# Where a fused decoder trunk gates and sums its output weights: one stage earlier, with three small moves in the attention

## The chip, the cores and the metric

The kernel runs on one core of one Trainium2 chip. The metric is the device time of one execution in microseconds (us). Three runs of the kernel before took 1230.39, 1235.14 and 1230.96 us; the median is 1230.96 us.

## What is computed

One decoder layer on x (1024 tokens x 1024 channels, float32): an adaLN-modulated RMSNorm, one combined input projection, two gated linear attentions side by side (HGRN2 with 8 heads, GLA with 4), a projection of each, a sigmoid gate on each, their sum, an output projection with a gate, a residual and a last RMSNorm.

```python
h = rms_norm(x, norm_w) * (1.0 + scale) + shift        # shift, scale, gate: silu(c) @ ada_w + ada_b
hq, hf, hi, hz, gq, gk, gv, gz, ga, mg = split(h @ w_in)
y_h = hgrn2_branch(hq, hf, hi, hz, lb, hgrn_norm_w)    # S_t = diag(f_t) S + (1 - f_t) i_t^T, norm, * silu(hz)
y_g = gla_branch(gq, gk, gv, gz, ga, ...)              # the same with alpha = sigmoid(W2 W1 x + b)^(1/16)
mg = sigmoid(mg)                                       # two gates per channel
merged = mg[0] * (y_h @ w_branch[0]) + mg[1] * (y_g @ w_branch[1])
x = x + gate * (merged @ w_out)
return rms_norm(x, final_norm_w)
```

The `gate` of the last line but one is a row over output channels, so the kernel multiplies it into the columns of `w_out` ahead of the product.

## The kernel before

**Arithmetic.** Every product is done in three matmuls on float32r parts: high times high, high times low, low times high. A tensor's high part is a rounding copy on ACT (`CAST` in the rows), its low part the difference, taken on DVE. Large projections use a Strassen-like scheme of seven products on half-size blocks, in the order `PRODUCTS = (1, 2, 5, 3, 6, 7, 4)`; weights of products 5, 6, 3 and 7 are sums of blocks.

**First two thirds.** After the norm, a stream of projections runs on TensorE (L541 and its neighbours), and the attention heads are woven in beside it: a head is a Python generator, and each `yield n` lets about n further units of stream matmuls be issued ahead of the next step of the head. In `attention` (L657) DVE prepares `xb` (L673 to L679), `yield 3` follows, then 32 pairs of score matmuls (L683). `inverse_root` (L957) splits a row of sums of squares into high and low parts (L197 on DVE is the low part) and multiplies both with ones (L964, L965). A second track prepares the weight sums (`ws`, L1200) and the factors of the activations (`fx`) in device memory.

**Last stages.** `last_stages` (L1388) runs four stages b = 0 to 3: the gate projection that goes with branch 1 (b = 0), the other gate (b = 1), the product of branch 1 (b = 2) and of branch 0 (b = 3). A stage is 7 products, a product is 4 pairs (i = 0 to 3), a pair is 12 matmuls (L1342) of 128 x 128 by 128 x 512. Weights come as "duos", two per product: loaded from device memory on SP's queue (L1273 for sums, L1277 for blocks of `w_in` or `w_branch`), cast on ACT (L1284), low part on DVE (L1285). `ahead` keeps duos loaded four and prepared two ahead. Activation factors are built by L1262 (ACT) and L1263 (DVE). Results leave PSUM as snapshots on ACT (L1314, L1316) and sums on DVE (L1329). The gate sigmoids (L1413) are stored through POOL's queue (L1414); put_gate0 (L1418) does the same without a store.

**Output weights.** `load_wy` (L1465) loads four 128 x 2 x 512 tiles of `w_out` (a half, kk), `gate_wy` (L1473) multiplies a tile by the gate, `sum_wy` (L1482) adds two, and `keep_wy` (L1468) stores a result, 512 KB each, through POOL's queue. `at` maps (stage, product, pair) to what is issued behind that pair. Before, both halves are in stage 1: half 0 is loaded behind product 2, gated in product 5, summed in product 3, half 1 loaded behind product 3, gated in product 6, summed in product 7; the tiles are freed at the last sum of their half.

**What sets the order.** Each engine works through its instructions in order. The tile framework orders them within an engine by its own scheduling, unless an instruction is kept in program order. All these tiles live in 46 equal slots of a FIFO (`N_SLOTS`): a slot freed is reused by the tile that asks next after all slots freed before it, and a load into it waits for the slot's last reader. PSUM banks of 512 columns are handed on through a list `R` (class Banks, L1289), too; before the last stages two 1024-column tiles are lent to it.

Of the kernel before, what the change touches and what calls it, by code (L numbers as in the profile page):

```python
# [15 lines left out]
P = 128  # L16
D = 1024
# [66 lines left out]
def hybrid_trunk_kernel(  # L84
# [20 lines left out]
    def dtile():  # L105
        cnt[0] += 1
        return ps_d.tile([P, T], F32, tag="d", name=f"pd{cnt[0]}")
# [548 lines left out]

    def attention(q, k, f, v, vo, V, post):  # L657

# [20 lines left out]
        TT(X[:, :, :, 4], X[:, :, :, 5], f4[:, :, :, 1], M)  # L679
        yield 3  # L680
        for b in range(32):
# [80 lines left out]
        grow(32)  # L762
        yield 7

# [192 lines left out]
    def inverse_root(dst, sq, n):  # L957

        hi, lo = split(sq)
        for half in range(2):  # L960
            sl = slice(half * 512, half * 512 + 512)
# [7 lines left out]
    def gla_attention(h):  # L969
# [16 lines left out]
        nc.gpsimd.tensor_add(sq[0], sq[0], sq[1])  # L986
        yield 2.5
        rst = sq[1]
        inverse_root(rst, sq[0], 256)
        for half in range(4):  # L990
# [94 lines left out]
    def hgrn_attention(h):  # L1085
# [4 lines left out]
        def post(vh, half, po):  # L1090
            if half == 0:
# [6 lines left out]
        yield from attention(st.pop(("q", h)), st.pop(("k", h)), st.pop(("f", h)), lambda: st[("v", h // 4)],  # L1098
                             h % 4 * P, P, post)
        if h % 4 == 3:  # L1100
# [7 lines left out]
        if h == 7:  # L1108
            yield 2
            rst = S.get([T])  # L1110
            inverse_root(rst, ssq[0], D)
            S.free(ssq[0])
            rst_h[0] = rst
# [356 lines left out]
    def gate_wy(kk, n):  # L1470
        kh, f = ((0, 0), (0, 1), (1, 0), (1, 1))[n]
        t = wy[kh, f]
        nc.vector.tensor_mul(t, t, gate_b[0][:, f * 512:f * 512 + 512].unsqueeze(1).to_broadcast([P, 2, 512]))  # L1473
        for p, at_ in X_OF.items():
# [5 lines left out]
    def sum_wy(kk, n):  # L1480
        p, dst, other = ((7, (0, 0), (0, 1)), (5, (0, 1), (1, 1)), (6, (1, 1), (0, 0)), (3, (1, 0), (1, 1)))[n]
        nc.vector.tensor_add(wy[dst], wy[dst], wy[other])  # L1482
        keep_wy(p, kk, *dst)
        if n == 3:
            S.free(*wy.values())
            wy.clear()

# [97 lines left out]

    for kk, (pa, pb) in enumerate(((5, 3), (6, 7))):
        after(1, 2 if kk == 0 else 3, 3, lambda kk=kk: load_wy(kk))
        for n in range(4):
            after(1, pa, n, lambda kk=kk, n=n: gate_wy(kk, n))
            after(1, pb, n, lambda kk=kk, n=n: sum_wy(kk, n))  # L1590

# [89 lines left out]
    S.free(*h_hi, *h_lo)  # L1681
    for _ in range(2):
        pd = dtile()
        R.lend([pd[:, 0:512], pd[:, 512:1024]])
    last_stages()
# [30 lines left out]
```

## Time and profile before

| | |
|---|---|
| runs | 1230.39, 1235.14, 1230.96 us |
| profiled execution | 1230.16 us, span 1228.3 us |
| mean granted TensorE clock | 0.993 |
| busy: PE, DVE, ACT, POOL | 1187.6, 791.6, 547.1, 123.7 us |
| DMA packets | 183.51 MB, 149 GB/s in the mean |
| `wo` stores (L1468) | 14 x 512 KB |
| gatings, sums of the output weights | 8 x 1.22 us from 904.2 us on, 8 x 1.225 us from 919.0 us on |

The profile names an instruction by its line, its engine and the tiles it writes and reads (`b` is any slot tile, `pd`, `pm` and `sc_ps` are PSUM, `ws`, `wo`, `fx`, `gate`, `yg`, `yh` tensors in device memory). A row of the timeline has start, duration, engine, line, operation, tiles, count, and in brackets how long the engine was idle before it and what ended that. Stage 0 begins beside the last attention head at 806.85 us, stage 1 begins at 899.33 us and its product 7 at 966.05 us.

### The profile page before, as it was taken

How to read it: one execution, taken by the hardware profiler on the slowest of the kernel's cores; microseconds unless marked ns; L12 is line 12 of the kernel's file. 1: busy time of each engine (PE TensorE's matmuls, PEld its weight loads, DVE VectorE, ACT ScalarE, POOL GpSimd, SP SyncE). 2: the span in 40 equal slices, each digit the busy share in tenths (PEclk: the TensorE clock that was granted, in tenths of full speed). 3: DMA queues.
4: the chain of work that ended last, by engine and by line, in shares of the span. 5: the costliest groups of instructions: out<-in, count | busy, mean ns of one | idle time of the engine just before them, and what ended most of it. 6: DMA issues, size and time to landing. Idle time of an engine off the chain costs nothing.

```text
span 1228.3 us, 20868 instructions
## 1 busy us (share of the span) xinstructions
PE 1187.6 (97%) x8579; PEld 984.7 (80%) x8579; DVE 791.6 (64%) x1245; ACT 547.1 (45%) x797; POOL 123.7 (10%) x215
## 2 busy tenths in 40 slices
PE   6999999999999999999999999999999699999997
PEld 3777889899898888788878878877888488878886
DVE  5636344774938465787774276785435666988994
ACT  5547723444444243324422334457632454544554
POOL 4100000202111112022010101011111000000000
PEclk9999999999999999999999999999999799999999
DMA  9714001845453367265151111245579736435533
GB/s 325 265 69 137 18 19 35 277 136 199 136 164 121 105 207 237 72 197 180 53 188 53 52 47 58 80 154 175 183 251 356 259 135 210 153 103 171 162 105 128
DMA packets 130961, 183.51 MB, mean 149 GB/s; under 512 B 7467, under 2 KB 97633, under 8 KB 130866
## 3 DMA queue, kind: packets, MB, share of 16 engines
q1 hardware_dynamic: 117250, 136.87, 35.4%
q0 software_dynamic: 13568, 45.31, 9.6%
q8 instruction: 67, 1.10, 0.4%
q14 instruction: 28, 0.23, 0.1%
q10 hardware_dynamic: 48, 0.01, 0.0%
HBM read 132.87 MB, written 49.28 MB: 148 GB/s over the span
## 4 chain that ended last, share of the span: by engine, by line
PE 51%; issue 29%; DVE 6%; POOL 3%; ACT 3%; DMA 3%; POOLq 0%; SPq 0%; DVEq 0%; ACTq 0%
PE pd L541 14%; PE pd L1342 7%; PE sc_ps L1342 4%; PE pm L1342 3%; PE pd L1517 3%; PE pd L643 2%; PE pd L645 2%; PE pd L644 2%; PE sc_ps L1517 2%; PE pd L352 1%; PE pm L848 1%; PE pm L1517 1%; PE pm L829 1%; PE pm L850 1%; POOL gate L1414 1%
## 5 line engine op out<-in xcount | busy, mean ns | idle before, releaser
L541 PE MATMUL pd<-b,b 128*128 128x512 f32 x1632 | 387.8, 394 | 0.0
L541 PEld LDWEIGHTS pd<-b,b 128*128 128x128 f32 x1632 | 302.3, 188 | 65.2 <-issue 1.4
L1342 PE MATMUL pd<-b,b 128*128 128x512 f32 x720 | 173.6, 392 | 2.4 <-DVE b L953 1.5
L1342 PEld LDWEIGHTS pd<-b,b 128*128 128x128 f32 x720 | 134.2, 188 | 33.3 <-DVE b L953 1.9
L197 DVE TENSOR_TENSOR b<-b,b 128x1024 fp32r<-128x1024 f32 (+2 forms) x89 | 99.1, 1124 | 83.4 <-ACT b L196 66.1
L196 ACT CAST b<-b 128x1024 fp32r<-128x1024 f32 (+2 forms) x89 | 82.9, 948 | 92.2 <-DVE b L1198 14.4
L1285 DVE TENSOR_TENSOR b<-b,b 128x1024 fp32r<-128x1024 f32 x56 | 68.4, 1224 | 52.2 <-ACT b L1284 19.6
L1342 PE MATMUL sc_ps<-b,b 128*128 128x512 f32 x324 | 81.8, 401 | 12.9 <-DVE b L1329 12.2
L1284 ACT CAST b<-b 128x1024 fp32r<-128x1024 f32 x56 | 58.3, 1049 | 75.5 <-PE pd L1342 19.1
L1342 PEld LDWEIGHTS sc_ps<-b,b 128*128 128x128 f32 x324 | 61.9, 193 | 27.4 <-DVE b L1329 12.6
L600 PE MATMUL pd<-b,b 128*128 128x256 f32 x256 | 74.2, 290 | 0.0
L1263 DVE TENSOR_TENSOR b<-b,b 128x1024 fp32r<-128x1024 f32 x48 | 59.5, 1254 | 21.7 <-ACT b L1262 14.3
L602 PE MATMUL pd<-b,b 128*128 128x256 f32 x256 | 72.5, 283 | 0.0
L601 PE MATMUL pd<-b,b 128*128 128x256 f32 x256 | 72.4, 283 | 0.0
L1342 PE MATMUL pm<-b,b 128*128 128x512 f32 x300 | 72.1, 389 | 0.0
L1262 ACT CAST b<-b 128x1024 fp32r<-128x1024 f32 x48 | 50.0, 1049 | 38.5 <-PE pd L1342 17.0
L1342 PEld LDWEIGHTS pm<-b,b 128*128 128x128 f32 x300 | 56.3, 188 | 11.7
L352 PE MATMUL pd<-b,b 128*128 128x512 f32 x192 | 53.2, 409 | 1.7 <-ACT b L196 0.9
L1200 POOL DMA_DIRECT2D ws<-b x64 | 34.6, 541 | 192.6 <-DVE b L1194 87.3
L643 PE MATMUL pd<-b,b 128*128 128x512 f32 x128 | 51.3, 401 | 0.0
L735 ACT COPY xb<-b 128x512 f32<-128x512 f32 x48 | 29.4, 620 | 48.2 <-PE sc_ps L715 26.3
L644 PE MATMUL pd<-b,b 128*128 128x512 f32 x128 | 49.9, 390 | 0.0
(285 smaller groups left out, 1965.4 us busy)
## 6 DMA issues: line engine op xcount, KB each, us to landing
b<-in_w_in_dram SPq DMA_DIRECT2D x66, 512.0 KB, 4.2
ws<-b POOLq DMA_DIRECT2D x64, 256.0 KB, 3.5
b<-ws SPq DMA_DIRECT2D x32, 512.0 KB, 4.1
b<-in_x_dram SPq DMA_DIRECT2D x16, 512.0 KB, 5.9
b<-in_ada_w_dram SPq DMA_DIRECT2D x32, 256.0 KB, 7.0
b<-in_w_branch_dram SPq DMA_DIRECT2D x16, 512.0 KB, 4.2
b<-h SPq DMA_DIRECT2D x14, 512.0 KB, 4.0
wo<-b POOLq DMA_DIRECT2D x14, 512.0 KB, 7.0
```

The source lines that it names most:

```text
L196: nc.scalar.copy(hi, src)
L197: nc.vector.tensor_sub(lo, src, hi.bitcast(F32))
L352: nc.tensor.matmul(accs[f], wg(a, d, f), b[d][:, half * 512:half * 512 + 512], start=(d == 0 and n == 0), stop=(d == KT - 1 and n == 2))
L541: nc.tensor.matmul(ps[0:w, th * 512:(th + 1) * 512], a[:, k, 0:w], b[:, th * 512:(th + 1) * 512], start=(k == 0 and n == 0), stop=(k == KT ...
L600: nc.tensor.matmul(o, lh, hi[:, k % 4, :], start=(k == 0), stop=False)
L601: nc.tensor.matmul(o, lh, lo[:, k % 4, :], start=False, stop=False)
L602: nc.tensor.matmul(o, ll, hi[:, k % 4, :], start=False, stop=(k == KT - 1))
L643: nc.tensor.matmul(o, lh, hi[:, k % 2, :], start=(k == 0), stop=False)
L644: nc.tensor.matmul(o, lh, lo[:, k % 2, :], start=False, stop=False)
L1285: nc.vector.tensor_sub(lo, t, hi.bitcast(F32))
L1342: nc.tensor.matmul(o, a[:, sl], c, start=(p in (1, 5) and kt == 0 and n == 0), stop=(kt == 3 and n == 2), skip_group_check=True)
L1517: nc.tensor.matmul(o, a, b, start=(p in (1, 5) and kt == 0 and n == 0), stop=(kt == 3 and n == 2), skip_group_check=True)
```

## The change

Four edits. The kernel's lines behind the split in inverse_root move down by one, those behind `gate_wy` by two and more.

1. Output weights: half 0 is loaded behind product 3, pair 0, of stage 0, gated in product 6 and summed in product 7 of stage 0; its tiles are freed behind the first pair of stage 1. Half 1 is loaded behind product 1, pair 2, of stage 1, gated in product 5 and summed in product 6, freed behind the last pair of product 7. Gatings and sums are kept in program order.
2. The two PSUM tiles are lent to `R` in reversed order.
3. `attention` gets an argument `lead`: heads 1 and 5 of HGRN issue their scores after `yield 4` and take `yield 6` in place of 7 later.
4. `inverse_root` is a generator with `yield 1` behind its split; GLA's `yield 2.5` ahead of it becomes 1.5.

```diff
--- before.py
+++ after.py
@@ -654,7 +654,7 @@
         return h_hi[k], h_lo[k]
 
 
-    def attention(q, k, f, v, vo, V, post):
+    def attention(q, k, f, v, vo, V, post, lead=3):
 
 
 
@@ -677,7 +677,7 @@
         TT(X[:, :, :, 1:4:2], q4[:, :, :, 2:4], f4[:, :, :, 2:4], M)
         TT(X[:, :, :, 2:6:3], X[:, :, :, 1:4:2], f4[:, :, :, 1:3], M)
         TT(X[:, :, :, 4], X[:, :, :, 5], f4[:, :, :, 1], M)
-        yield 3
+        yield lead
         for b in range(32):
             ch, j = b // 4, b % 4
             nc.tensor.matmul(sc_ps[32 * j:32 * j + 32, ch * P:ch * P + 80], k[:, b * 32:b * 32 + 32], xb[:, b, :],
@@ -760,7 +760,7 @@
         grow(16)
         keep(32)
         grow(32)
-        yield 7
+        yield 10 - lead
 
 
         k16, q16 = kept[16]
@@ -957,6 +957,7 @@
     def inverse_root(dst, sq, n):
 
         hi, lo = split(sq)
+        yield 1
         for half in range(2):
             sl = slice(half * 512, half * 512 + 512)
             pn = mtile()
@@ -984,9 +985,9 @@
         yield from attention(qk.pop(("q", h)), qk.pop(("k", h)), alphas[h], lambda: v, 0, 256, post)
         S.free(*v)
         nc.gpsimd.tensor_add(sq[0], sq[0], sq[1])
-        yield 2.5
+        yield 1.5
         rst = sq[1]
-        inverse_root(rst, sq[0], 256)
+        yield from inverse_root(rst, sq[0], 256)
         for half in range(4):
             sl = slice(half * 256, half * 256 + 256)
             for vh in range(2):
@@ -1096,7 +1097,7 @@
                                            y[0][:, sl], ALU.mult, ALU.mult)
 
         yield from attention(st.pop(("q", h)), st.pop(("k", h)), st.pop(("f", h)), lambda: st[("v", h // 4)],
-                             h % 4 * P, P, post)
+                             h % 4 * P, P, post, 4 if h % 4 == 1 else 3)
         if h % 4 == 3:
             S.free(*st.pop(("v", h // 4)))
         put_act(yh_d, h, y[0])
@@ -1108,7 +1109,7 @@
         if h == 7:
             yield 2
             rst = S.get([T])
-            inverse_root(rst, ssq[0], D)
+            yield from inverse_root(rst, ssq[0], D)
             S.free(ssq[0])
             rst_h[0] = rst
 
@@ -1470,7 +1471,8 @@
     def gate_wy(kk, n):
         kh, f = ((0, 0), (0, 1), (1, 0), (1, 1))[n]
         t = wy[kh, f]
-        nc.vector.tensor_mul(t, t, gate_b[0][:, f * 512:f * 512 + 512].unsqueeze(1).to_broadcast([P, 2, 512]))
+        tc.keep_in_program_order(nc.vector.tensor_mul(
+            t, t, gate_b[0][:, f * 512:f * 512 + 512].unsqueeze(1).to_broadcast([P, 2, 512])))
         for p, at_ in X_OF.items():
             if at_ == (kh, f):
                 keep_wy(p, kk, kh, f)
@@ -1479,11 +1481,12 @@
 
     def sum_wy(kk, n):
         p, dst, other = ((7, (0, 0), (0, 1)), (5, (0, 1), (1, 1)), (6, (1, 1), (0, 0)), (3, (1, 0), (1, 1)))[n]
-        nc.vector.tensor_add(wy[dst], wy[dst], wy[other])
+        tc.keep_in_program_order(nc.vector.tensor_add(wy[dst], wy[dst], wy[other]))
         keep_wy(p, kk, *dst)
-        if n == 3:
-            S.free(*wy.values())
-            wy.clear()
+
+    def drop_wy():
+        S.free(*wy.values())
+        wy.clear()
 
     def load_w4(p):
         w4_raw[p] = [S.get([2, 512]) for _ in range(2)]
@@ -1583,11 +1586,12 @@
             for z in W4.pop(p):
                 S.free(*z)
 
-    for kk, (pa, pb) in enumerate(((5, 3), (6, 7))):
-        after(1, 2 if kk == 0 else 3, 3, lambda kk=kk: load_wy(kk))
+    for kk, (lead, first, then) in enumerate((((0, 3, 0), (0, 6), (0, 7)), ((1, 1, 2), (1, 5), (1, 6)))):
+        after(*lead, lambda kk=kk: load_wy(kk))
+        after(*((1, 1, 0) if kk == 0 else (1, 7, 3)), drop_wy)
         for n in range(4):
-            after(1, pa, n, lambda kk=kk, n=n: gate_wy(kk, n))
-            after(1, pb, n, lambda kk=kk, n=n: sum_wy(kk, n))
+            after(*first, n, lambda kk=kk, n=n: gate_wy(kk, n))
+            after(*then, n, lambda kk=kk, n=n: sum_wy(kk, n))
 
     def last_of_11():
         combine(4, "22", "22", "11")
@@ -1679,9 +1683,8 @@
     stream.hooks[1, 4] = begin_2
     stream.go()
     S.free(*h_hi, *h_lo)
-    for _ in range(2):
-        pd = dtile()
-        R.lend([pd[:, 0:512], pd[:, 512:1024]])
+    lent = [dtile() for _ in range(2)]
+    R.lend([pd[:, i * 512:i * 512 + 512] for pd in lent[::-1] for i in range(2)])
     last_stages()
     out_stage()
```

On ACT, around the start of product 7 of stage 1, the rows before are these (L1284 casts weights, `b604` is a tile loaded from `w_branch` for stage 2, `b569` the `ws` tile of product 7; L1314 and L1316 are snapshots of PSUM, the number in `pd185` is that of the bank):

```order
L1314 COPY b563_8440<-pd184_7440 128x512
L1284 CAST b576_8539<-b566_8463 128x1024
L1314 COPY b563_8440<-pm195_7961 128x512
L1284 CAST b592_8633<-b578_8543 128x1024
L1284 CAST b618_8801<-b604_8721 128x1024
L1284 CAST b584_8585<-b569_8497 128x1024
L1316 ACTIVATE b579_8557<-sc_ps_72 128x512
L1418 ACTIVATE b580_8560<-b579_8557 128x512
L1284 CAST b596_8673<-b586_8589 128x1024
```

With the change the same place reads (lines one higher):

```order
L1285 CAST b576_8546<-b570_8486 128x1024
L1315 COPY b567_8463<-pd185_7441 128x512
L1285 CAST b584_8593<-b573_8516 128x1024
L1315 COPY b567_8463<-pm195_7969 128x512
L1285 CAST b592_8641<-b578_8550 128x1024
L1317 ACTIVATE b579_8564<-sc_ps_72 128x512
L1419 ACTIVATE b580_8567<-b579_8564 128x512
L1285 CAST b596_8677<-b586_8597 128x1024
...
L1285 CAST b618_8801<-b604_8721 128x1024
```

The cast of `b604` has moved from ahead of product 7's cast to 16 rows behind it.

On DVE, in products 6 and 7 of stage 0, the rows before are (L1329 sums a snapshot and a bank, L1263 is the low part of an activation factor, L1285 of a weight):

```order
L1329 TENSOR_TENSOR b510_8041<-b510_8041,sc_ps_72 128x512
L1329 TENSOR_TENSOR b514_8065<-b514_8065,pd185_7441 128x512
L1285 TENSOR_TENSOR b519_8092<-b504_8002,b518_8091 128x1024
L1329 TENSOR_TENSOR b517_8086<-b517_8086,pd185_7441 128x512
L1263 TENSOR_TENSOR b524_8116<-b516_8071,b522_8114 128x1024
L1285 TENSOR_TENSOR b526_8137<-b513_8050,b525_8136 128x1024
L1329 TENSOR_TENSOR b475_7821<-pd184_7440,b475_7821 128x512
L1285 TENSOR_TENSOR b529_8174<-b520_8095,b528_8173 128x1024
L1329 TENSOR_TENSOR b475_7821<-pd184_7440,b475_7821 128x512
L1285 TENSOR_TENSOR b534_8211<-b527_8140,b533_8210 128x1024
```

and now (L1474 is a gating, L1484 a sum of output weights; `b497` to `b500` are the four tiles of half 0):

```order
L1474 TENSOR_TENSOR b498_7950<-b498_7950,b378_6016 128x1024
L1330 TENSOR_TENSOR b518_8076<-b518_8076,pd184_7440 128x512
L1474 TENSOR_TENSOR b499_7952<-b499_7952,b378_6016 128x1024
L1330 TENSOR_TENSOR b521_8099<-b521_8099,pd184_7440 128x512
L1474 TENSOR_TENSOR b500_7954<-b500_7954,b378_6016 128x1024
L1330 TENSOR_TENSOR b475_7821<-pd185_7441,b475_7821 128x512
L1264 TENSOR_TENSOR b527_8130<-b519_8081,b525_8128 128x1024
L1264 TENSOR_TENSOR b528_8131<-b520_8082,b526_8129 128x1024
L1484 TENSOR_TENSOR b497_7948<-b497_7948,b498_7950 128x1024
L1330 TENSOR_TENSOR b475_7821<-pd185_7441,b475_7821 128x512
L1484 TENSOR_TENSOR b498_7950<-b498_7950,b500_7954 128x1024
L1286 TENSOR_TENSOR b530_8156<-b517_8061,b529_8155 128x1024
```

Gatings stand between the bank sums of product 6, sums of output weights between those of product 7, and the low parts of weights (L1286) come behind two sums.

On PE, at HGRN's head 1, the rows before are (L541 is the stream's projection, L683 the scores, whose two matmuls differ in the column group):

```order
L541 MATMUL pd123_4543<-b9_147,b273_4495 128x512 x2
L683 MATMUL sc_ps_72<-xb_142,b277_4535 32x80 x32
L541 MATMUL pd123_4543<-b10_148,b272_4494 128x512 x2
L541 MATMUL pd123_4543<-b18_156,b272_4494 128x512 x2
L541 MATMUL pd123_4543<-b10_148,b273_4495 128x512 x2
L541 MATMUL pd123_4543<-b11_149,b272_4494 128x512 x2
```

and now:

```order
L541 MATMUL pd123_4543<-b9_147,b273_4495 128x512 x2
L541 MATMUL pd123_4543<-b10_148,b272_4494 128x512 x2
L541 MATMUL pd123_4543<-b18_156,b272_4494 128x512 x2
L541 MATMUL pd123_4543<-b10_148,b273_4495 128x512 x2
L683 MATMUL sc_ps_72<-xb_142,b277_4535 32x80 x32
L541 MATMUL pd123_4543<-b11_149,b272_4494 128x512 x2
```

L683 stands three rows of two matmuls later.

## The prediction

> **What bounds the kernel now.** I read the page first (busy shares and the 40 slices), then the list of what each engine waited for, then the timeline around the largest wait.
>
> ```profile
> PE 1187.6 (97%) x8579; PEld 984.7 (80%) x8579; DVE 791.6 (64%) x1245; ACT 547.1 (45%) x797; POOL 123.7 (10%) x215
> ...
> PE   6999999999999999999999999999999699999997
> ...
> PEclk9999999999999999999999999999999799999999
> ```
>
> TensorE (PE) is busy for 97% of the span of 1228.3 us. A change that keeps the number of matmuls, as this one does, can only win where PE waits or where its clock is low. The slices show one such place besides the two ends: slice 32 of 40 (952 to 983 us), 6 tenths busy and 7 tenths of the clock. The list of waits says for whom.
>
> ```profile
> PE sc_ps L1342 <- DVE b L1329: 12.2, 1, 12.2
> PE pm L219 <- DVE b L210: 7.2, 4, 4.0
> ...
> PE sc_ps L683 <- DVE xb L679: 1.7, 2, 0.9
> PE pd L1342 <- DVE b L953: 1.5, 1, 1.5
> ...
> PE pm L964 <- DVE b L197: 0.5, 1, 0.5
> PE pd L1342 <- DVE b L1434: 0.5, 1, 0.5
> ```
>
> The columns are total us, how often, longest. The 7.2 us at L219 belong to the start, which the change leaves alone. Of the rest the edits aim at four rows: 12.2, 1.7, 1.5 and 0.5, together 15.9 us.
>
> **The 12.2 us.** These rows of the timeline (start, duration, engine, line) show it backwards from PE:
>
> ```profile
> 924.06 1.27 SPq L1273 DMA_DIRECT2D b<-ws  x2
> ...
> 947.74 0.86 SPq L1277 DMA_DIRECT2D b<-in_w_branch_dram  x1
> 949.20 1.00 SPq L1277 DMA_DIRECT2D b<-in_w_branch_dram  x1
> ...
> 959.41 1.99 ACT L1284 CAST b<-b 128x1024 fp32r<-128x1024 f32 x2 [12.92 <-DMA b<-in_w_branch_dram]
> ...
> 963.04 2.36 DVE L1285 TENSOR_TENSOR b<-b,b 128x1024 fp32r<-128x1024 f32 x2 [6.57 <-DMA wo<-b]
> 965.31 0.68 DVE L1329 TENSOR_TENSOR b<-b,sc_ps 128x512 f32<-128x512 f32 x1
> ...
> 966.05 5.49 PE L1342 MATMUL sc_ps<-b,b 128*128 128x512 f32 x12 [12.16 <-DVE b L1329]
> ```
>
> PE stands at the first matmul of product 7 of stage 1 until 966.05. VectorE (DVE) gave it the low part of that product's weights and the freed bank (L1329) only after 963.04; ScalarE (ACT) had cast two weight tiles at 959.41 after idling 12.92 us for a load from w_branch, issued at 947.74 to 949.20. The order of ACT (section on the change) shows which two: first the tile of w_branch for stage 2, then the tile of product 7. The second's load was issued by 925.3; it stood behind the first. The load came late because it took buffers that the gating and sums of the output weights held.
>
> In the changed order that cast of product 7 stands 16 rows ahead of the w_branch cast. So this wait's mechanism goes, 12.16 us. What is late next: product 7 then needs a ws tile, which SP loads ahead of the in_w_in tiles, and its DVE part, ahead of which stand no sums of the second half any more.
>
> The clock goes with it:
>
> ```profile
> 956.00:962.00 6.00, 0.00 (x0) 0.00 (x0) 0.47 (x1) 2.48 (x3) 0.16 (x1) 0.67 1.04 413
> 962.00:970.00 8.00, 3.95 (x9) 3.17 (x10) 5.33 (x6) 3.07 (x5) 0.00 (x0) 0.50 0.32 98
> ...
> 966.05 5.49 PE sc_ps L1342 x12
> 971.54 5.57 PE pd L1342 x24
> 977.10 2.72 PE pm L1342 x12
> ```
>
> In the windows the third number from the right is the granted clock, 0.67 and then 0.50; in the chain 12 matmuls take 5.49 us after the wait and 2.72 later, and 24 take 5.57 for 5.44. Loss 2.77 + 0.13 = 2.90. **Term: 12.16 + 2.90 = 15.06 us.**
>
> The Trainium skill ("TensorE: Matmul & The Clock Gate", Part 1: The HAM clock gate) says that the clock halves after an idle window of about 3.4 us and returns after about 3.4 us of sustained work. The trace agrees on the half (0.50); by the page's window the loss would be about 1.7 us (an estimate), by the rows it is 2.90, and the rows decide; by the page the sum below would be 1215.1 in place of 1213.9.
>
> **Scores a step later (1.7 us).** L683 of heads 1 and 5 is put behind six more matmuls of L541 (1.36 us at the 0.2267 us that 2.72 / 12 gives).
>
> ```profile
> 496.38 1.31 PE L683 MATMUL sc_ps<-xb,b 128*32 128x80 f32 x64 [0.88 <-DVE xb L679]
> ...
> 717.26 1.31 PE L683 MATMUL sc_ps<-xb,b 128*32 128x80 f32 x64 [0.85 <-DVE xb L679]
> ...
> 501.34 0.45 DVE L711 TENSOR_TENSOR xb<-xb,tot 128x256 f32<-128x256 f32 x1
> ...
> 504.69 0.89 PE L715 MATMUL sc_ps<-xb,b 128*32 128x48 f32 x64
> ```
>
> The wait is 0.88 at head 1 and the other 0.85 at head 5: both are shorter than 1.36 and vanish. The next step on these heads, L715, stays where it was; its DVE input ends at 501.8 and it starts at 504.69, so nothing takes the wait's place. **Term: 1.73 us.**
>
> **The inverse root.** L964 of head 7 gets two matmuls (0.45 us) ahead of it where it waited 0.48 by its row (0.5 in the list). For GLA the same edit leaves PE's order as it was (2.5 becomes 1.5 and 1). What L964 starts comes 0.45 us later in PE's order, and no wait in the list hangs on it. **Term: 0.45 us.**
>
> **The bank.** The 1.5 us row is PE waiting for L953 before the first matmuls of the last stages. Reversing the two lent tiles changes which of them is handed on first, but the bank handed on first was free long before in either order, and the next one waits for L953 in both. So I cost it at nothing: the 1.5 us stay. If the reversal did what it says, at most 1.5 us.
>
> **What the change adds.** The first half's four loads, four gatings, four sums and seven stores (eight of each of the first three in all, as before) move to stage 0. Their prices:
>
> ```profile
> L1482 DVE TENSOR_TENSOR b<-b,b x8: 1218/1225/1226, 919.0 to 954.1; 128x1024 f32<-128x1024 f32 x8
> ...
> yh<-b POOLq DMA_DIRECT2D x16, 256.0 KB, 4.3
> ...
> DMA to landing us min/median/max: 2.3/2.8/6.6
> ...
> DMA to landing us min/median/max: 3.1/7.0/8.8
> ```
>
> The first landing row is that of the gate stores (L1414), the second that of the wo stores (L1468). In stage 0 DVE gets 8 × 1.225 = 9.8 us. There it is 6.07 of 10 us busy (first row below), so the work fits beside PE; the cost lies in two places where a buffer is freed just before it is used, both since the four loaded tiles take four of the 46 slots there:
>
> ```profile
> 880.00:890.00 10.00, 9.97 (x45) 7.92 (x44) 6.07 (x7) 4.29 (x6) 1.86 (x4) 1.00 0.69 210
> ...
> 852.92 0.55 POOL L916 DMA_DIRECT2D yh<-b  x1
> ...
> 860.73 1.52 PE L1342 MATMUL pd<-b,b 128*128 128x512 f32 x6
> ...
> 879.70 0.54 POOL L1414 DMA_DIRECT2D gate<-b  x1 [2.26 <-ACT b L1413]
> ...
> 888.35 2.88 PE L1342 MATMUL pd<-b,b 128*128 128x512 f32 x12
> ```
>
> First, at product 3 of stage 0, two ACT casts wait for a yh store to land. They stand ahead of the copy that frees a bank for PE. Store issued 852.92, landed 857.2 by the median, then 1.05 + 1.05 + 0.59 = 859.9; PE wants the bank at 860.3. Slack 0.4; were the store to take the wo stores' 7.0 us, 2.3 late, with other work between about 2.0. Second, at product 4 (888.35), the weights' cast waits for a gate store, issued about 880.4 and landed 883.2 by the median; behind it stand on DVE a bank sum, a gated sum (1.225) and the low part (1.22), done about 887.9, wanted after two matmuls at 888.8. Slack 0.9; with 6.6 us 0.5 late, with 8.8 us 2.7 late. Both together: between 0 and 2.0 + 2.7 = 4.7. The gain end is −0.5, were the L1434 wait to move with the DVE work. I take +1.0, since the medians of both are under the slack and only the tails of the rows are over it.
>
> A page's price for the same stores: the Trainium skill ("DMA: Bandwidth & Descriptors", Anatomy of one DMA — SWDGE (gpsimd) path) fits 2.0 us plus bytes over 436e3 per us, so 2.6 us for 256 KB and 3.2 for 512 KB. The row gives 2.8 for the gate stores, which agrees, but 7.0 for the wo stores, which does not; by the page the +1.0 would be 0.
>
> **Sum.** 1230.16 (profiled execution: span 1228.3 and 1.9 around it) − 15.06 − 1.73 − 0.45 + 1.0 = 1213.9. The three runs have the median 1230.96, 0.8 above the profiled one and 0.6 above the fastest. I give **1214.0**.
>
> **Rivals.**
> A. New waits in stage 0 of 3 to 8 us: one of the two stores above lands at its row's maximum with the queue fuller than before. For: the wo stores' median is 7.0, and they now run beside the gate stores. Against: DMA share 0.69 there. One wait over some 3 us may cost the clock again (the wait of 12.16 cost 2.90). 1216.5 to 1222; chance 0.12.
> B. The wait before product 7 is a matter of bytes, not of ACT's order: in these windows DMA is full,
>
> ```profile
> 930.00:940.00 10.00, 10.00 (x46) 8.28 (x45) 3.96 (x4) 1.68 (x3) 1.31 (x3) 1.00 1.03 393
> 940.00:950.00 10.00, 10.00 (x46) 8.29 (x45) 7.08 (x6) 1.05 (x1) 1.59 (x3) 1.00 1.01 368
> ```
>
> and product 7's own weights come late. Whole: 1230.16 − 1.73 − 0.45 = 1228.0; half of the 15.06 left: 1220.4. Against: half of the output weights' loads and stores, 4 × 0.5 + 7 × 0.5 MB, has left this stretch. Chance 0.08, of it 0.05 for the whole.
> C. The small edits don't do what they say: the two scores and the root keep their waits. 1213.9 + 2.2 = 1216.1; chance 0.04.
> D. Slower than before. POOL's queue takes the wo stores of the first half and the gate stores in one stretch (872 to 905 us, 7 × 0.5 + 12 × 0.25 = 6.5 MB); a load on SP's queue that waits for the store of a sum holds back the in_w_in loads behind it, for product 2 of stage 1.
>
> ```profile
> 910.21 1.98 PE L1342 MATMUL sc_ps<-b,b 128*128 128x512 f32 x8
> ...
> b<-in_w_in_dram SPq DMA_DIRECT2D x24, 256.0 KB, 4.5
> ...
> L1468 POOL DMA_DIRECT2D wo<-b x14: 531/531/537, 911.6 to 955.6; - x14
> ```
>
> PE wants them at 910.2; less 4.5 of landing, 1.05 and about 1.2 they must be issued by 903.5. The last sum but one of the first half ends on DVE about 889.7, its store is out 0.5 later and lands 7.0 after that, so I expect 897, and it decides from a backlog of 6.5 us; each us over that is one lost, plus 2.9 of clock. It outweighs the 17.2 us won from 6.5 + 17.2 − 2.9 = 20.8 us on. Against: before, the same queue took 14 × 0.5 MB in the 44 us from 911.6 on without waiting longer than 8.8 us for one. Chance 0.05 (1237 and above); a backlog of 14 us would give 1224.
>
> **How the numbers follow.** My forecast 0.71 (1211 to 1216.5), A 0.12, B 0.08, C 0.04, D 0.05. The range 1211 to 1222 holds the forecast, A and C and the part of B that leaves half: 0.71 + 0.12 + 0.04 + 0.03 = 0.90. Without A 0.78 would be left, under 8 in 10. A measurement here can tell about 0.5% (6.2 us), so faster means below 1224.8: forecast, A, C and half B, 0.90; same 0.05 (B whole); slower 0.05 (D).
>
> **What would show it.** Right: no PE wait above 1 us after 900 us, the slice's clock at 9, twelve matmuls at product 7 in 2.72 us; no rows L683 among PE's waits for two heads; the wait for L953 still near 1.5. Wrong: a PE wait in stage 0 ended by an ACT copy or DVE low part (A); DMA share 1.0 and a ws load landing after 950 (B); SP's load of in_w_in issued after 903 (D).

## The result, and the profile after

The changed kernel takes **1217.56 us** (median of 1216.46, 1215.71, 1218.80 and 1218.65) against 1230.68 us for the kernel before (four runs, 1230.22 to 1235.14): ratio **0.9884**, 95% interval 0.9856 to 0.9912. The profiled execution took 1216.46 us, span 1214.8 us. One of the nine runs of the kernel before beside E5 to E8 took 5243 us and is left out of their ratios.

The page after has the same lines as before at another height: busy shares, the slices of PE and its granted clock.

```profile
PE 1184.1 (97%) x8579; PEld 982.6 (81%) x8579; DVE 790.9 (65%) x1245; ACT 546.9 (45%) x797; POOL 123.8 (10%) x215
...
PE   5999999999999999999999999999999999999997
...
PEclk9999999999999999999999999999999999999999
```

The dent in slice 32 is gone, in PE and in its clock. DVE and ACT work as long as before to within 1 us: nothing was saved on them. PE's list of waits after (total us, how often, longest):

```profile
PE pm L219 <- DVE b L210: 8.3, 4, 4.0
...
PE pd L1343 <- ACT b L1414: 2.1, 2, 1.8
PE pd L1343 <- DVE b L953: 1.5, 1, 1.5
...
PE pd L1343 <- DVE b L1435: 0.4, 1, 0.4
```

Against before: the 12.2 us of L1329 (now L1330), the 1.7 us of L683 and the 0.5 us of L964 are gone; the 1.5 us of L953 is as it was; the row of an ACT sigmoid (L1413, now L1414) has grown from 0.3 to 2.1 us, by a new wait of 1.8; and the start (L219) took 8.3 in place of 7.2 us. Product 7 of stage 1 begins here, in PE's timeline (start, duration, engine, line):

```profile
951.94 2.88 PE L1343 MATMUL pm<-b,b 128*128 128x512 f32 x12
954.66 2.88 PE L1343 MATMUL sc_ps<-b,b 128*128 128x512 f32 x12
957.38 5.60 PE L1343 MATMUL pd<-b,b 128*128 128x512 f32 x24
```

No bracket, so no idle time: the 12 matmuls at 954.66 are those that before started at 966.05 after 12.16 us of waiting. They take 2.72 us from start to the next start (5.49 before).

PE runs the same 8579 matmuls in both executions, nearly all in the same order, so the start of the same matmul can be compared from place to place. From start to start a short wait costs 0.1 to 0.3 us more than its bracket says, because the profile's modelled end of a matmul lies behind the next one's start. What each place adds:

| place on PE | after minus before, us | the prediction's term |
|---|---|---|
| start, first 140 us | +1.2 | none |
| scores of heads 1 and 5 | −0.99, −0.94 | −0.88, −0.85 |
| wait for L793 at 834 us, 1.0 for 0.7 | +0.24 | none |
| inverse root of head 7 | −0.68 | −0.45 |
| stage 0, product 3 (copy) | +0.45 | with the next two, +1.0 |
| stage 0, product 7 (881.87 before: a start 0.3 late, gone) | −0.31 | |
| stage 0, product 4 (sigmoid) | +2.0 | (0 to 4.7) |
| stage 1, product 7, wait and clock | −15.05 | −15.06 |
| at the last matmul | −13.9 | −16.2 |

The rows add up to −14.1; the 0.2 left is spread over the rest. Behind the last matmul another 0.2 is lost.

**The new wait.** PE, ACT and POOL around it, of the changed kernel:

```profile
884.49 2.00 ACT L1285 CAST b<-b 128x1024 fp32r<-128x1024 f32 x2 [3.04 <-issue]
886.39 0.62 ACT L1414 ACTIVATE b<-b 128x512 f32<-128x512 f32 x1
...
892.22 0.60 ACT L1414 ACTIVATE b<-pd 128x512 f32<-128x512 f32 x1 [0.76 <-DMA gate<-b]
```

```profile
879.41 0.54 POOL L1415 DMA_DIRECT2D gate<-b  x1 [0.93 <-ACT b L1414]
...
887.31 0.54 POOL L1415 DMA_DIRECT2D gate<-b  x1 [3.01 <-ACT b L1414]
```

```profile
892.87 3.02 PE L1343 MATMUL pd<-b,b 128*128 128x512 f32 x12 [1.82 <-ACT b L1414]
```

From below: PE waits for a bank that the sigmoid at 892.22 reads; that sigmoid waits for a `gate` store to land, since it writes into the slot which that store reads; the store was issued at 887.31 and so took some 4.8 us; it could not be issued earlier, because its own sigmoid (886.39) stood on ACT behind two weight casts; and the first of those casts started only when an earlier gate store, issued at 879.41, had landed (884.42, after 5.0 us). For that last step the bracket names no releaser, but the times fit here and in two other runs: the casts start at 884.49, in E7 at 885.49 behind a landing at 885.42, in E12 at 886.46 behind one at 886.40. Two store landings in series, linked by ACT's order. The windows of that stretch (length, busy times and counts, granted clock, DMA share, GB/s) show why the landings are slow:

```profile
884.00:888.00 4.00, 4.00 (x20) 3.30 (x19) 3.63 (x5) 2.53 (x3) 0.99 (x3) 1.00 1.05 348
888.00:892.00 4.00, 3.05 (x14) 2.20 (x12) 4.00 (x5) 2.10 (x3) 1.69 (x4) 1.00 1.08 394
892.00:896.00 4.00, 3.13 (x14) 2.60 (x15) 0.54 (x1) 0.90 (x2) 1.38 (x3) 1.00 0.99 367
896.00:900.00 4.00, 4.00 (x19) 3.33 (x18) 1.22 (x1) 1.84 (x3) 1.08 (x2) 1.00 1.01 395
```

The DMA share (last but one) is 0.99 to 1.08; before it was 0.69 at 880 to 890. The clock stays at 1.00 behind this wait.

### The profile page after: what moved, and what is told of

It reads as the page before. It is cut to its first block, busy times and chain, and to the rows that moved or that the text cites. A ratio compares the mean times of both kernels' runs of the same rounds, so it can differ in the third digit from the quotient of the medians.

```text
span 1214.8 us, 20860 instructions
## 1 busy us (share of the span) xinstructions
PE 1184.1 (97%) x8579; PEld 982.6 (81%) x8579; DVE 790.9 (65%) x1245; ACT 546.9 (45%) x797; POOL 123.8 (10%) x215
## 4 chain that ended last, share of the span: by engine, by line
PE 61%; issue 23%; DVE 3%; ACT 3%; POOL 2%; DMA 1%; POOLq 0%; ACTq 0%; DVEq 0%
PE pd L541 19%; PE pd L1343 9%; PE sc_ps L1343 5%; PE pm L1343 5%; PE pd L1520 3%; PE pd L643 2%; PE pd L644 2%; PE pd L645 2%; PE sc_ps L1520 2%; PE pm L848 1%; PE pd L352 1%; PE pm L829 1%; PE pm L850 1%; PE pm L1520 1%; PE sc_ps L352 1%
## 5 line engine op out<-in xcount | busy, mean ns | idle before, releaser
L541 PE MATMUL pd<-b,b 128*128 128x512 f32 x1632 | 387.4, 394 | 0.0
L541 PEld LDWEIGHTS pd<-b,b 128*128 128x128 f32 x1632 | 302.4, 188 | 64.8 <-issue 1.4
L1343 PE MATMUL pd<-b,b 128*128 128x512 f32 x720 | 173.7, 392 | 4.3 <-ACT b L1414 2.1
L1343 PEld LDWEIGHTS pd<-b,b 128*128 128x128 f32 x720 | 133.7, 188 | 35.7 <-ACT b L1414 3.2
L197 DVE TENSOR_TENSOR b<-b,b 128x1024 fp32r<-128x1024 f32 (+2 forms) x89 | 98.9, 1122 | 83.1 <-ACT b L196 65.4
L1286 DVE TENSOR_TENSOR b<-b,b 128x1024 fp32r<-128x1024 f32 x56 | 68.3, 1224 | 66.9 <-ACT b L1285 52.3
L1285 ACT CAST b<-b 128x1024 fp32r<-128x1024 f32 x56 | 58.3, 1050 | 73.9 <-PE pd L1343 20.6
L1343 PE MATMUL sc_ps<-b,b 128*128 128x512 f32 x324 | 79.4, 391 | 1.0 <-ACT scT L793 1.0
L1343 PEld LDWEIGHTS sc_ps<-b,b 128*128 128x128 f32 x324 | 60.3, 188 | 14.6 <-ACT scT L793 1.4
L1343 PE MATMUL pm<-b,b 128*128 128x512 f32 x300 | 72.1, 389 | 0.0
L1263 ACT CAST b<-b 128x1024 fp32r<-128x1024 f32 x48 | 49.9, 1050 | 41.2 <-PE pd L1343 16.0
L1343 PEld LDWEIGHTS pm<-b,b 128*128 128x128 f32 x300 | 56.3, 188 | 11.7
```

What stands on the lines that cost most here:

```text
L197: nc.vector.tensor_sub(lo, src, hi.bitcast(F32))
L541: nc.tensor.matmul(ps[0:w, th * 512:(th + 1) * 512], a[:, k, 0:w], b[:, th * 512:(th + 1) * 512], start=(k == 0 and n == 0), stop=(k == KT ...
L1286: nc.vector.tensor_sub(lo, t, hi.bitcast(F32))
L1343: nc.tensor.matmul(o, a[:, sl], c, start=(p in (1, 5) and kt == 0 and n == 0), stop=(kt == 3 and n == 2), skip_group_check=True)
```

## The experiments

Each ratio is to the kernel before on the same chip. E1 to E4 take the change apart, the others go for the new wait and the scatter of the runs. Letters in the expectations stand for the theories that the text beside them names.

**E1. Only ACT's order at product 7** (kernel before, with one cast kept in program order; all DMA as before). Theory O: the order of two casts on ACT makes the 12.2 us; rival B: the bytes do.

```diff
-        nc.scalar.copy(hi, t)
+        (tc.keep_in_program_order if duo == (2, 1, 1) else id)(nc.scalar.copy(hi, t))
```

> The kernel before, with one cast (the second w_branch tile of product 1 of stage 2) kept in program order: ACT then casts product 7's tile first, and DVE takes its low part first; all loads, stores, gatings and sums stay where they were, so the bytes are the same. Theory O (the order on ACT made the 12.16 us): what is late next is DVE, whose last sum ran at 954.11 after a store's landing, then two low parts of 1.14 and the bank sum of 0.68, so PE starts product 7 at about 958.3 and waits 4.4 us in place of 12.16; 1230.7 - 7.8 = 1222.9 if the clock still loses 2.9, 1220.0 if not. Rival B (bytes: the weights themselves land too late because DMA is full): the wait stays above 10 us and the time within 1228 to 1231.

Measured: 1222.70 us, 0.9932 (0.9915 to 0.9949). PE's wait, and the DVE row that ends it:

```profile
PE sc_ps L1342 <- DVE b L1329: 4.0, 1, 4.0
```

```profile
954.61 1.23 DVE L1482 TENSOR_TENSOR b<-b,b 128x1024 f32<-128x1024 f32 x1 [3.54 <-DMA wo<-b]
```

```profile
958.76 5.40 PE L1342 MATMUL sc_ps<-b,b 128*128 128x512 f32 x12 [3.98 <-DVE b L1329]
```

With the same bytes in the same stretch, 12.2 became 4.0 us: 8.2 us were order, and B falls. The other 4.0 have a second cause: on DVE a sum of output weights (L1482) waits 3.54 us for a `wo` store and holds up the low part behind it. The change takes both away, because its sums of that half are not there any more. The clock cost nearly as much behind 3.98 us (12 matmuls take 5.24 us to the next start at 964.00, in place of 2.72) as behind 12.16 us (5.49).

**E2. Only edit 1** (output weights).

```diff
-    for kk, (pa, pb) in enumerate(((5, 3), (6, 7))):
-        after(1, 2 if kk == 0 else 3, 3, lambda kk=kk: load_wy(kk))
+    for kk, (lead, first, then) in enumerate((((0, 3, 0), (0, 6), (0, 7)), ((1, 1, 2), (1, 5), (1, 6)))):
+        after(*lead, lambda kk=kk: load_wy(kk))
...
```

(with the rest of edit 1: gatings and sums in program order, freeing as in the change)

> Only the first edit: the output weights' gating and sums moved, the rest as before. Theory: this edit carries all of the 15.06 us and also the new wait of 1.8 us at product 4 of stage 0, so 1230.7 - 15.06 + 1.8 = 1217.5 and the waits for L679 at heads 1 and 5 stay (0.9 and 0.9). Rival: part of the gain belongs to the other edits (bank, scores), then this is above 1219.5.

Measured: 1220.21 us, 0.9907 (0.9890 to 0.9924); 2.7 us above the expected 1217.5. Of these, 0.75 belong to the kernel before, which takes 1231.45 us in its runs beside this one and not 1230.7. The 12.2 us are gone, but PE's list has a wait at product 3 of stage 0 that the whole change lacks:

```profile
PE pd L1342 <- ACT b L1314: 2.0, 1, 2.0
PE pd L1342 <- ACT b L1413: 1.9, 2, 1.6
```

ACT at that place, edit 1 alone:

```profile
859.04 2.00 ACT L1284 CAST b<-b 128x1024 fp32r<-128x1024 f32 x2 [3.75 <-DMA yh<-b]
861.06 1.28 ACT L965 ACT_TABLE_LOAD   x1
862.36 1.26 ACT L965 ACTIVATE b<-pm,eps_t 128x512 f32<-128x512 f32 x2
863.51 0.58 ACT L1314 COPY b<-pd 128x512 f32<-128x512 f32 x1
```

and in the changed kernel:

```profile
857.29 2.00 ACT L1285 CAST b<-b 128x1024 fp32r<-128x1024 f32 x2 [3.07 <-DMA b<-ws]
859.20 0.57 ACT L1315 COPY b<-pd 128x512 f32<-128x512 f32 x1
859.79 1.28 ACT L966 ACT_TABLE_LOAD   x1
861.09 1.27 ACT L966 ACTIVATE b<-pm,eps_t 128x512 f32<-128x512 f32 x2
```

With edit 1 alone the inverse root's table load and activations (about 2.5 us) stand ahead of the copy that frees PE's bank; with the root's `yield 1` they stand behind it. E3, which has no edit 1, shows the same order (copy at 855.28, table load at 855.88), so it goes with edits 3 and 4. Without those 2.5 us the copy would have ended at about 861.6, before PE had finished the matmuls ahead (862.1): the order decides. Here the 2.0 us also cost clock:

```profile
862.11:865.52 3.41, 1.41 (x7) 1.15 (x7) 0.38 (x1) 3.37 (x6) 0.00 (x0) 1.00 0.19 77
865.52:868.93 3.41, 3.41 (x10) 2.63 (x9) 0.46 (x1) 3.41 (x5) 0.00 (x0) 0.50 0.02 5
868.93:872.34 3.41, 3.41 (x16) 2.83 (x16) 3.41 (x4) 1.42 (x2) 0.07 (x1) 1.00 0.16 26
```

3.41 us at half clock are 1.7 us lost. In this execution the root's split would thus have saved 3.7 us beside its own 0.45. The times don't bear out that size: the profiled execution is the slowest of the four (1221.96 us, the others 1219.99 to 1220.29), and by the medians edit 1 alone is 2.5 to 2.7 us above the whole change, of which the scores (1.93) and the root (0.45) account for 2.4. That edit 1 alone brings the wait in this order is shown; its price over many executions is not.

**E3. Only the scores and the inverse root.**

```diff
-        yield 3
+        yield lead
...
+        yield 1
```

> Only the two edits on the attention: scores of heads 1 and 5 a step later, inverse root in two steps. Theory: 0.88 + 0.85 + 0.45 = 2.2 us go, nothing takes their place: 1228.5, and the 12.2 us wait at product 7 of stage 1 stays. Rival C (a later step waits instead): 1230.7 and a new wait on the same heads.

Measured: 1229.47 us, 0.9986 (0.9976 to 0.9995), 2.0 us less than before. By matmul starts the scores give 0.99 and 0.94 us and the root 0.40. The rows L683 and L964 are gone from PE's waits; the largest one stays (`PE sc_ps L1343 <- DVE b L1330: 12.8, 1, 12.8`). The two edits do what they say here; for the root that does not hold in every execution (see below).

**E4. Only the bank.**

```diff
+    lent = [dtile() for _ in range(2)]
+    R.lend([pd[:, i * 512:i * 512 + 512] for pd in lent[::-1] for i in range(2)])
```

> Only the reversed order in which the two PSUM tiles are lent. Theory: nothing, 1230.7 within a run's scatter, and PE's wait for L953 is 1.5 us as before, since the first bank used gets the tile that is long free in either order. Rival (the edit does what it says): the wait for L953 is gone, 1229.2.

Measured: 1231.27 us, 0.9999 (0.9989 to 1.0008); `PE pd L1342 <- DVE b L953: 1.5, 1, 1.5` is still there. Worth nothing.

**E5. The changed kernel once more,** for the scatter between its runs (1215.7 to 1218.8).

> The changed kernel once more, unaltered, as the one the next three are compared with. Its four runs lay at 1215.71, 1216.46, 1218.65 and 1218.80. Theory T: the two groups differ in one wait, at product 3 of stage 0 (pair 2), where the copy of a bank stands behind two casts that wait for a yh store to land; when the store lands about 2 us later PE waits 2 us and loses 1.7 us of clock, as in the run of the weights alone. Then its runs fall again into two groups about 2.5 us apart, and a profile of the upper group shows the wait. Rival: the groups come from the start of the kernel (the first waits on loads), then the profile shows it there.

Measured: 1217.76 us (1215.65 to 1218.89), 0.9887 (0.9873 to 0.9901). The theory that the longer executions are those with the product-3 wait falls: this profiled execution (1217.60 us) has none there. It lost 1.6 us near 646 us, where PE never waits. Windows of this execution, and then of the first profiled execution of the same program:

```profile
644.00:648.00 4.00, 4.00 (x9) 2.61 (x10) 1.23 (x1) 1.61 (x2) 0.00 (x0) 0.63 0.09 19
648.00:652.00 4.00, 4.00 (x18) 3.27 (x17) 0.00 (x0) 0.00 (x0) 0.00 (x0) 0.95 0.41 116
```

```profile
644.00:648.00 4.00, 4.00 (x16) 2.74 (x16) 1.23 (x1) 1.63 (x2) 0.00 (x0) 1.00 0.06 13
648.00:652.00 4.00, 4.00 (x20) 3.30 (x19) 0.00 (x0) 0.00 (x0) 0.00 (x0) 1.00 0.43 122
```

PE is busy for the whole of both, but 9 matmuls fit where 16 did, at a granted clock of 0.63. Such a loss comes in one execution and not in another of the same program. E11's profiled execution has one at the same place; what stands ahead of it is told in the last section.

**E6. Two ACT casts of product 6 kept in program order,** so that the copy at product 3 stands ahead of them, and **E7. The four sum stores of half 0 on SP's queue.** For E7 theory Q says that the gate stores land late because they share POOL's queue with the 512 KB stores; theory S, that all transfers share the 16 engines.

```diff
-        nc.scalar.copy(hi, t)
+        (tc.keep_in_program_order if duo[:2] == (0, 6) else id)(nc.scalar.copy(hi, t))
```

```diff
-        nc.gpsimd.dma_start(w4_d[p][kk], wy[kh, f].rearrange("p a f -> p (a f)"))
+        (nc.sync if kk == 0 and p in SUMS else nc.gpsimd).dma_start(w4_d[p][kk], wy[kh, f].rearrange("p a f -> p (a f)"))
```

> The changed kernel with the casts of product 6's two weight tiles in stage 0 kept in program order: the bank's copy at product 3, pair 2, then stands ahead of them and waits for no store. Theory T: the lower group alone remains, all runs within 1 us of 1216, and no wait for the copy. Rival: the casts now come late for product 6 (a wait there of 0.5 to 2 us), or the two groups stay.

> The changed kernel with the four stores of the first half's sums issued on SP's queue in place of POOL's; ACT, DVE and PE keep their orders. Theory Q: the 1.8 us wait at product 4 of stage 0 comes from the gate store that shares POOL's queue with wo stores and takes 4.8 us to land; alone it lands in about 3, and the wait falls below 0.6, time 1.3 us less than the changed kernel. Rival R: the order on ACT makes it (the sigmoid stands behind two weight casts and starts 2.3 us late); then the landing moves little and the wait stays within 0.5 us of 1.8.

Measured: E6 1216.21 us, 0.9879 (0.9865 to 0.9893), within the interval of the change, the sigmoid wait as before (1.9 us) and the scatter too (1215.4 to 1218.1); the copy does stand ahead of the casts, and no wait for it is left. E7 1218.36 us, 0.9890 (0.9874 to 0.9906), with a longer wait:

```profile
PE pd L1343 <- ACT b L1414: 3.3, 2, 3.0
```

```profile
888.00:892.00 4.00, 4.00 (x18) 3.00 (x16) 4.00 (x5) 1.96 (x4) 0.59 (x2) 1.00 1.04 378
892.00:896.00 4.00, 0.98 (x3) 0.83 (x3) 1.54 (x2) 0.76 (x2) 1.55 (x3) 0.81 1.05 406
```

The gate store issued at 888.31 had no sum store ahead of it on POOL's queue any more and still took 6.0 us. Q falls; the share of the 16 engines stayed at 1.04. Not all of E7's loss is this wait: its profiled execution also waits 2.4 us for L953, for 1.5, and loses clock behind both.

**E8. E6 and E7 together.**

> Both edits: the casts of product 6 in program order and the sums' stores on SP's queue. If T and Q hold, the sum of the two: about 1214.6, with all runs within 1 us, and no PE wait above 1.6 us after 800 us. If only T holds, 1216; if neither, as the changed kernel.

Measured: 1218.10 us, 0.9901 (0.9883 to 0.9918); sigmoid wait 3.2 us in all. It behaves like E7; nothing was added up.

**E9. One cast of product 4 kept in program order,** which brings the late sigmoid ahead of the second cast. Theory R: the store is late because it is issued late; S: because it lands late.

```diff
+        (tc.keep_in_program_order if duo == (0, 4, 0) else id)(nc.scalar.copy(hi, t))
```

> The changed kernel with one cast kept in program order, that of the first weight tile of product 4 of stage 0: on ACT the gate sigmoid of product 7, pair 1, then stands behind one weight cast in place of two and starts about 0.9 us earlier; PE, SP and POOL keep their orders. Theory R (ACT's order sets when the gate store is issued, and the next sigmoid into that buffer waits for its landing): PE's wait of 1.5 to 1.8 us at product 4 shrinks by 0.9, to 0.6 to 0.9. Rival S (16 full DMA engines pace the landing whenever it is issued): the store lands at the same time and the wait stays within 0.3 us.

Measured: 1216.41 us, 0.9874 (0.9859 to 0.9888). The wait seems to shrink, and another stands just ahead of it:

```profile
889.17 2.55 PE L1343 MATMUL pd<-b,b 128*128 128x512 f32 x10 [0.47 <-DVE b L1286]
891.55 1.07 PE L1343 MATMUL pm<-b,b 128*128 128x512 f32 x4
893.54 3.03 PE L1343 MATMUL pd<-b,b 128*128 128x512 f32 x12 [0.92 <-ACT b L1414]
```

The cast put back made its low part late. By matmul starts the stretch gains 0.14 us net. The store went out 0.9 us earlier relative to PE and landed only 0.1 us earlier, after 5.6 us: this speaks for S.

**E10. Half 0 a product earlier** (gated in product 3, summed in product 6), to get its stores away before product 4, and **E11. E10 with E6's order.**

```diff
-            after(*first, n, lambda kk=kk, n=n: gate_wy(kk, n))
-            after(*then, n, lambda kk=kk, n=n: sum_wy(kk, n))
+            after(*(first if kk else (0, 3)), n if kk else 2 + n // 2, lambda kk=kk, n=n: gate_wy(kk, n))
+            after(*(then if kk else (0, 6)), n, lambda kk=kk, n=n: sum_wy(kk, n))
```

> The changed kernel with the first half gated in product 3 (pairs 2 and 3) and summed in product 6 of stage 0, so that its stores leave about 11 us earlier and not in the full stretch from 888 to 900 us. Theory S (the landing of the gate stores is slow because all DMA engines are full there): the share of DMA between 888 and 896 falls below 0.9, the gate store lands in about 3 us in place of 4.8 and the wait at product 4 falls below 0.7, time 1.2 us less than the changed kernel. Theory R alone: the sigmoid still stands behind two casts, the wait stays at 1.3 or more.

> The same with the bank's copy at product 3 ahead of product 6's casts. If both places are cured no PE wait above 1.6 us is left after 800 us and the time is about 1214.5 in its median, the best so far; the scatter of 2 to 3 us between runs, which a clock dip near 646 us without any wait makes, stays. Rival: four gatings in a row on DVE delay product 6's low parts, a new wait of 1 us or more at product 6.

Measured: 1221.19 us, 0.9919 (0.9906 to 0.9931), and 1222.54 us, 0.9930 (0.9917 to 0.9943): both slower than the change. The sigmoid wait grew to 2.8 and 3.2 us. The stretch did not empty; windows of E10:

```profile
884.00:888.00 4.00, 4.00 (x20) 3.30 (x18) 1.83 (x2) 1.16 (x2) 0.80 (x2) 1.00 1.07 390
888.00:892.00 4.00, 3.33 (x14) 2.13 (x13) 1.83 (x2) 1.98 (x3) 0.00 (x0) 1.00 1.08 372
```

Between 884 and 896 us the stores moved 2.1 MB, for 2.9 in the changed kernel, but the loads on SP's queue 2.2 MB for 1.6. That these loads moved up because their slots came free earlier is argued, not shown. The profiled executions of both also have a longer wait for L953 (2.3 and 2.4 us), so part of their loss is not this one.

**E12. The four sum stores of half 0 kept behind product 4's gate stores,** the sums where they are.

```diff
-        keep_wy(p, kk, *dst)
+        after(0, 4, 2, lambda: keep_wy(p, kk, *dst)) if kk == 0 else keep_wy(p, kk, *dst)
```

(the four stores also kept in program order)

> The changed kernel with the four stores of the first half's sums kept behind the gate stores of product 4 of stage 0 (pairs 0 to 2), so that 2 MB of stores leave the full stretch from 884 to 896 us and run after 897. Theory S (all 16 DMA engines are full there, and that paces the gate store's landing): the landing of the gate store of product 7, pair 1, falls from 4.8 us to 3 or less, and PE's wait at product 4 from 1.5 to 1.8 to below 0.6; about 1.3 us less than the changed kernel, 1216.3 beside 1217.7. Rival D: the buffers of these tiles come free about 10 us later, and a load behind them is late in stage 1: a new PE wait there, longer than what was won. Rival R (ACT's order of casts and sigmoid): the wait stays above 1.3.

Measured: 1216.27 us (1213.91 to 1217.77), 0.9871 (0.9854 to 0.9889), as expected.

```profile
PE pd L1343 <- ACT b L1414: 0.8, 2, 0.5
```

```profile
888.00:892.00 4.00, 4.00 (x19) 3.31 (x18) 4.00 (x5) 2.95 (x5) 0.62 (x2) 1.00 0.84 257
892.00:896.00 4.00, 3.51 (x16) 2.58 (x15) 2.52 (x3) 0.92 (x3) 1.54 (x3) 1.00 0.53 198
```

Share 0.84 and 0.53 for 1.08 and 0.99; the gate store took 2.9 us (issued 889.29, the sigmoid behind it free at about 892.2) for 4.8, though issued later relative to PE; by matmul starts the stretch gains 1.33 us. The median of the gate stores' landings, on the rows of this line, went from 4.6 us in the changed kernel to 3.0. The stores put off then take 8.4 to 10.5 us, and nothing on PE waits for them. S stands against Q and R. It is the lowest ratio of all, but its interval overlaps the change's: that it is faster than the change isn't settled by the times, only the shorter wait is.

## Why the prediction held, point by point

Predicted were 1214.0 us in a range of 1211 to 1222; measured were 1217.56 us. Direction and range held; the forecast was 3.6 us low.

- **Wait and clock at product 7, 15.06 us:** measured 15.05. The step that went by ACT's order was right (E1) but carried the whole 12.16 us, where order is worth 8.2 and DVE's wait behind a `wo` store the other 4.0. The prediction touched on the second cause (no sums of the second half stand ahead of the DVE part any more) without pricing it; a change that only swapped the casts would have been forecast some 6 us too low (E1 took 8.75 us off, not 15.06).
- **Scores, 1.73 us:** 1.93 by matmul starts, here and in E3. Right.
- **Inverse root, 0.45 us:** 0.68 by matmul starts here, 0.40 in E3. The mechanism was right, that the whole wait goes was partly luck: of ten profiled executions with this edit three have no wait left (this one, E3 and E7), E6 has 0.2 us, and six have 0.4, E5's of the same program among them (`PE pm L965 <- DVE b L197: 0.4, 1, 0.4`); the four without the edit have 0.5 to 0.7. What it left out: the split also puts the copy at product 3 ahead of the root's work on ACT (E2), so the slack of 0.4 us there rested on this edit as well as on the store's landing.
- **Bank, nothing:** right (E4).
- **New waits, +1.0 us: the mis-sized term.** Measured 2.0 + 0.45 − 0.31 = 2.1. It lies inside the bounds of 0 to 4.7, at product 4 as named, and starts from the gate store and the cast that were named. What failed is the step "behind it stand on DVE a bank sum, a gated sum and the low part": the list of what stands behind the waiting cast left out ACT itself. There a sigmoid stood behind it, whose store is waited for by the next sigmoid, so the landing counts twice. And the price of one landing was the 2.8 us median of before, where the row after has 4.6. For the store that the prediction named the median was wrong already before: issued at 879.70, it landed at 884.36, after 4.7 us, at a DMA share of 0.95 (5.0 us after the change). The next one went from 3.0 us (issued 887.23, share 0.84) to 4.8 (share 1.07), in the stretch that the change fills with its own stores.
- **The start:** +1.2 us in this execution, which no term had; most of it stands in L219's row (8.3 for 7.2). It is scatter between executions: L219's row reads 6.5 to 8.3 in the 14 profiled ones, 7.5 in E5's of the same program.

Of the 2.6 us between the sum (1213.9) and the profiled execution (1216.46), 1.2 are the start and 1.1 the new waits; the rest is the balance of smaller differences; the median of the runs is 1.1 above that execution. E5 shows one way that an execution loses as much, the clock.

The rivals: A (new waits of 3 to 8 us) had the kind of the wait right, but the size was 2.1; E7 reaches 3.0 us in one wait. Its "over some 3 us" for a loss of clock was too high: 2.0 us cost 1.7 in E2. B fell with E1, C with E3. D (SP's queue held up by the stores' backlog) did come, to a point: the load of output weights issued at 890.92 had waited 6.4 us on SP for a sum's store. SP's issues later on:

```profile
902.00 0.92 SPq L1278 DMA_DIRECT2D b<-in_w_in_dram  x2
902.96 0.50 SPq L1274 DMA_DIRECT2D b<-ws  x1
903.57 7.42 SPq L1466 DMA_DIRECT2D b<-in_w_out_dram  x2
911.08 0.89 SPq L1274 DMA_DIRECT2D b<-ws  x2
```

The next one stands on SP from 903.57 to 911.0, for a gate store (`SPq L1466 <- DMA gate<-b: 6.5, 1, 6.5`), but the in_w_in loads had gone out at 902.0, 1.5 us ahead of the prediction's limit, and behind it are only ws loads for later products. PE waits for none of them. E12 issues the stores later still (902.4 to 904.6), and no PE wait follows there either.

What stays open: why the start varies by about 1 us, why the wait for L953 is 2.3 to 2.4 us in E7, E10 and E11 and 1.4 to 1.5 in the others, and whether E12 beats the change.

## To carry to other kernels

When an instruction on an in-order engine waits for a transfer, list everything behind it on **that** engine first, and follow each of those to the next transfer: landings in series are missed when only the other engine's queue is followed. A landing takes longer where the DMA engines are full, so a change that moves stores into a stretch also changes the price of the stores already there; a queue of their own (E7) or an earlier time (E10) didn't help, a later time when nothing waits (E12) did. A wait that one reordering removes may have a second one right behind it: E1 alone still waits 4.0 us.

## What the runs showed of the hardware that was not expected

- A loss of clock comes in whole windows. Call a stretch at a granted clock of 0.50 a spell. In the traces with several spells all of them begin on one raster of 3.41 us, fixed for the execution: in E7 at 812.53 and 894.45, which are 24 × 3.413 us apart. What counts is how much of a wait falls into one window. E2's 2.00 us lay whole in 862.11 to 865.52, and the next window ran at 0.50 (lines in E2). The changed kernel's 1.82 us fell on both sides of a boundary (raster counted back from its only spell, at the end, 1209.86), 1.37 and 0.45 us, and the clock stayed at 1.00:

```profile
889.01:892.42 3.41, 2.04 (x10) 1.34 (x8) 3.41 (x4) 2.30 (x4) 1.54 (x4) 1.00 1.07 402
892.42:895.83 3.41, 2.96 (x13) 2.46 (x14) 0.12 (x1) 0.53 (x2) 0.96 (x2) 1.00 0.99 359
```

  Over the 14 profiled executions, behind the start and ahead of the last 15 us, each window at full clock with 1.95 us of PE idle or more is followed by one at half (1.95 in E7, 2.00 in E2), and of those with 1.63 us (E6) or less only the two of E5 and E11 told below, where PE had not waited. So in these traces the edge lies between 1.63 and 1.95 us of idle in a window, and not at a length of the wait.
- The price is half of the time that PE works in such windows: 3.41 us behind E2's wait (1.7 us lost), 5.17 behind the 3.98 us of E1 (2.6) and 5.60 behind the 12.16 us (2.8). So waits of quite different length cost nearly the same. The Trainium skill ("TensorE: Matmul & The Clock Gate", Part 1: The HAM clock gate) puts the idle window at about 3.4 us. The traces agree on that length; but an idle time of 1.95 to 2.0 us within a window was enough here, and a loss of 1.7 us is that of the shortest spell alone.
- The clock can fall without any wait: 0.63 over 4 us at 644 us in E5, with PE busy throughout, and 1.00 in another execution of the same program. Ahead of that spell stand eight matmuls of L1062 and L1063 (640.82 to 644.93), which take about 0.53 us each from start to start, for 0.23 of the others; those of L1063 use one row of 128. The raster's window ahead of the spell, 641.59 to 645.01, holds all four of L1063, and so does the one in E11 (639.90 to 643.31); in none of the other twelve executions does one window hold them all, and none has this spell. That this sets it off is argued from these traces, not tested.
- One 256 KB store took 2.9 us at a DMA share of 0.84, 4.8 to 5.0 us at 1.05 to 1.08 and 6.0 us at 1.04, on the same queue. The share does not settle it alone: in the kernel before, the gate store issued at 892.16 took 5.1 us at a share of 0.71.
